# Pinning the weights' sums behind the evictions on VectorE, and issuing a row's end behind the next row's sum in the last product

## The chip, the core and the metric

The kernel runs on one core of one Trainium2 chip. The core has a matrix engine (PE, TensorE), three engines for elementwise work (DVE or VectorE, ACT or ScalarE, POOL or GpSimd), a queue for transfers (SP), an on-chip memory SBUF of 128 partitions, and PSUM, the memory into which PE writes its sums. Each engine works through its own instructions in the order in which they were laid out when the kernel was built; semaphores hold an instruction back until what it reads is there. The metric is the device time of one execution in microseconds, the median of the runs.

## What is computed

A decoder block with two attention branches, a gated merge, a SwiGLU feed-forward and a final RMSNorm, on 1024 tokens of width 1024. The change touches the feed-forward and the final norm alone:

```
h = rmsnorm(x, norm_ffn_g[l])
gu = h @ w_ffn_in[l]                                     # 1024 x 1024 times 1024 x 5632
x = x + (silu(gu[..., :D_FF]) * gu[..., D_FF:]) @ w_ffn_out[l]   # D_FF = 2816
return rmsnorm(x, norm_final_g)
```

## The kernel before, in words

All matrix products are made to float32 accuracy from three passes: each operand is split into a part `hi` and a remainder `lo`, and hi·hi, lo·hi and hi·lo are added in PSUM. `split` (L100 to L102) makes `hi` on ACT (L101) and then `lo = src - hi` on DVE or POOL (L102).

**The first feed-forward product** (L1002 to L1207) works in 22 feature blocks `f` of 128 columns. A block's gate weights `g` and up weights `u` are two rows of 128 x 1024 in SBUF, loaded by `load_f` (L921). A block needs four quarter products per output; a scheme of Strassen's kind makes them from seven products of half size, in the order of `SEQ`: A11, S2, A12, S3, S1, A22, S4. Here A11, A12 and A22 are halves of the loaded weights, and S1 to S4 are sums of them:

```
1028  V.tensor_add(S1, u, d["A22"])
1029  V.tensor_sub(S2, S1, d["A11"])
1030  V.tensor_sub(S3, d["A11"], u)
1031  V.tensor_sub(S4, d["A12"], S2)
```

These are "the weights' sums", four VectorE operations of 128 x 512 on SBUF per block. They are written in `prep`, which the loop calls four products ahead; so the sums of block f+1 stand in the code behind product S1 of block f and its eviction (L1082). Each product's weights are then split: `hi` on ACT into a tile `ahi`, `lo` on POOL into `alo`; there are six of each.

A product is twelve matmuls of 128 x 512 (four slices, three passes) on L1061. Its result is evicted by `product_out`: A11 by ACT (L1070), A12 by ACT as a Silu (L1076), and by DVE S2 (L1073), S3 (L1079), S1 (L1082), A22 (L1085, then the multiplication L1086) and S4 (L1090, then Silu on ACT L1091 and the multiplication L1092). Three PSUM banks take part: A11 and A12 add into `mm`; S2, S3 and A22 into `tr`; S1 and S4 into `big`. A later product of a bank adds to what the earlier one left there, and the earlier state has to be read first: S3 can't start before L1073 has read S2, nor A22 before L1079, nor S4 before L1082. Between the two there is one product of another bank.

After each odd block, `sums` (L1104 to L1107) makes four more sums on DVE, of the two blocks' activations, and SP stores them. In each odd block POOL also makes four sums of the second product's weights (`tsums`, L1123 to L1126), whose place is fixed.

**The second feed-forward product** (L1273 to L1302) runs in 77 units of twelve matmuls (L1277). The last of its seven passes (p = 6) finishes token rows 0 to 3: the last three units run row by row, nine matmuls a row; `evict` adds the result to the residual (L1261), `square` takes the sum of squares on ACT (L1220), and `finish` adds two halves of it (L1225), forms the inverse root on DVE (L97) and POOL (L98), scales one half of the row on ACT (L1229) and the other on DVE (L1230), and issues two stores (L1232).

**What sets the order.** A scheduler lays out each engine's instructions when the kernel is built, by its own estimates of when their operands are ready; so an instruction can stand earlier or later on its engine than in the code. `tc.keep_in_program_order(...)` around an instruction forbids that for it: it stays behind what the code issued before it on its engine.

Of the kernel before, what the change touches and what calls it, by code (L numbers as in the profile page):

```python
# [50 lines left out]
def block_kernel(ctx, tc, x, pos, g_mix, w_qk, w_v, q_scale, w_idx, w_gate, ikg, ikb, lams, sub_g, gate_b,  # L51
                 w_bdsa, w_bdiff, w_out, g_ffn, w_ffi, w_ffo, g_fin, out):
    nc = tc.nc
    V, A, G, T = nc.vector, nc.scalar, nc.gpsimd, nc.tensor
# [39 lines left out]
    def rsqrt(dst, ssq, n, eps):  # L94
        k = ssq.shape[-1]
        v = small.tile([P, NT], F32, name="rs_v")
        V.tensor_scalar(v[:, :k], ssq, 1.0 / n, eps, op0=OP.mult, op1=OP.add)  # L97
        G.tensor_tensor(dst, v[:, :k], nhalf[:, :k], op=OP.pow)  # L98

    def split(hi, lo, src, lo_eng):  # L100
        A.activation(hi, src, AF.Copy)  # L101
        lo_eng.tensor_sub(lo, src, hi.bitcast(F32))  # L102
# [676 lines left out]
    for h in range(4):  # L779
        for j, t in enumerate(ORDER):  # L780
            u = Unit()
# [5 lines left out]
    for m in range(8):  # L787
        prs = {}
        for j, t in enumerate(ORDER2):
            u = Unit()  # L790
# [9 lines left out]
    for i in range(len(units) + 9):  # L800
        if i < len(units) and units[i].first:
            u = units[i]
# [6 lines left out]
        for lag in range(10):  # L809
            if 0 <= i - lag < len(units):  # L810
                u = units[i - lag]
# [51 lines left out]
    class Space:  # L863
# [26 lines left out]
        def drop(self, *aps):  # L890
            for ap in aps:
                self.free += self.of.pop(id(ap))[1]
# [4 lines left out]
    def blk(early):  # L897
        if early:
            return b1p.tile([P, 2, 4, 512], F32R, name="blk", bufs=2)
        return b2p.tile([P, 2, 4, 512], F32R, name="blk", bufs=5)  # L900

    def row4(src):
        t = full()
        nc.sync.dma_start(t, bass.AP(tensor=src.tensor, offset=src.offset, ap=[[0, P], [1, D]]))
        return t
# [111 lines left out]
    def prep(n, early=False):  # L1017
        if n >= len(plan):
            return
        f, (a_, _, _) = plan[n]  # L1020
        if f not in src_:
            g, u = raws[f]
            src_[f] = dict(A11=g[:, :512], A12=g[:, 512:], A22=u[:, 512:], own=[g, u])
        d = src_[f]
        if a_[0] == "S" and "S2" not in d:
            S1, S2, S4 = (half_() for _ in range(3))
            S3 = u = d["own"][1][:, :512]
            V.tensor_add(S1, u, d["A22"])  # L1028
            V.tensor_sub(S2, S1, d["A11"])
            V.tensor_sub(S3, d["A11"], u)  # L1030
            V.tensor_sub(S4, d["A12"], S2)
            d.update(S1=S1, S2=S2, S3=S3, S4=S4)
            d["own"] += [S1, S2, S4]
        if early:
            t = W3.pool.tile([P, 1024], F32R, name="raw", bufs=2)
            hi, lo = t[:, :512], t[:, 512:]
        else:
            hi = arp.tile([P, 512], F32R, name="ahi", bufs=6)
            lo = arp.tile([P, 512], F32R, name="alo", bufs=6)
        split(hi, lo, d[a_], G)  # L1040
        wops[n] = hi, lo
        if a_ == "S4":
            drop(*d["own"])
# [93 lines left out]
    def load_u(n):  # L1137
        if n >= len(unit) or n in uraw:
            return
        p, j = unit[n]  # L1140
        a_, b_ = SEQ2[p]
        lo_, hi_ = slice(0, 512), slice(512, 1024)
        sa = {"A11": act_dr[2 * j][:, lo_], "A12": act_dr[2 * j + 1][:, lo_], "A22": act_dr[2 * j + 1][:, hi_],
              "S1": s_dr[j][0], "S2": s_dr[j][1], "S3": s_dr[j][2], "S4": s_dr[j][3]}[a_]
        sb = {"B11": w_ffo[2 * j][:, lo_], "B21": w_ffo[2 * j + 1][:, lo_], "B22": w_ffo[2 * j + 1][:, hi_],
              "T1": t_dr[j][0][:, lo_], "T3": t_dr[j][0][:, hi_], "T4": t_dr[j][1][:, lo_],
              "T2": t_dr[j][1][:, hi_]}[b_]
        t = uraw[n] = full()
        nc.sync.dma_start(t[:, :512], sa)
        nc.sync.dma_start(t[:, 512:], sb)  # L1150

    def split_u(n):
        if n >= len(unit) or n in uop:
            return
        if n % 2 == 0:
            ublk[n // 2] = blk(False).rearrange("p a b c -> p (a b c)").rearrange("p (n a c) -> p n a c", n=2, a=2)
        v = ublk[n // 2][:, n % 2]
        split(v[:, 0, :], v[:, 1, :], uraw[n], V)
        drop(uraw[n])
        uop[n] = v  # L1160

    banks, ev = [None] * 3, {}
    prep(0, True)
    prep(1, True)
    half1 = turn2("T2", 0)
    product(0)
# [10 lines left out]
    for n in range(2, 6):  # L1177
        prep(n)
# [30 lines left out]
    def x2_load():  # L1209
        for h in range(2):  # L1210
            v = blk(True).bitcast(F32).rearrange("p a b c -> p (a b c)").rearrange("p (r c) -> p r c", r=4)
            for r in R:
                x2[4 * h + r] = v[:, r, :]
                nc.sync.dma_start(x2[4 * h + r], x2_dr[4 * h + r])

    def square(i, u):
        if i not in sqs:
            sqs[i] = small.tile([P, 2], F32, name="ssq2")
        junk = half_()
        A.activation(junk, x2[i][:, u * 512:u * 512 + 512], AF.Square, accum_out=sqs[i][:, u:u + 1])  # L1220
        drop(junk)

    def finish(i):
        sq = sqs[i]
        V.tensor_add(sq[:, 0:1], sq[:, 0:1], sq[:, 1:2])  # L1225
        r = small.tile([P, 1], F32, name="rstd")
        rsqrt(r, sq[:, 0:1], D, EPS)

        A.activation(x2[i][:, :512], x2[i][:, :512], AF.Copy, scale=r)  # L1229
        V.scalar_tensor_tensor(x2[i][:, 512:], x2[i][:, 512:], r, gfin[:, 512:], op0=OP.mult, op1=OP.mult)  # L1230
        for u in range(2):
            nc.sync.dma_start(out[i * P:(i + 1) * P, u * 512:u * 512 + 512], x2[i][:, u * 512:u * 512 + 512])  # L1232

    def evict(p, r, X):
        L, H = slice(0, 512), slice(512, 1024)
        if p == 0:
            pA[r] = half_()
            A.activation(pA[r], X, AF.Copy)
        elif p == 1:
            V.tensor_add(x2[r][:, L], X, x2[r][:, L])  # L1240
            square(r, 0)
            G.tensor_mul(x2[r][:, L], x2[r][:, L], gfin[:, L])
        elif p == 2:
            u2[r] = half_()
            V.tensor_add(u2[r], X, pA[r])  # L1245
            G.tensor_add(u2[r], u2[r], x2[r][:, H])
        elif p == 3:
            u3[r] = half_()
            V.tensor_add(u3[r], X, pA[r])
            G.tensor_add(u3[r], u3[r], x2[4 + r][:, H])  # L1250
            G.tensor_add(pA[r], pA[r], x2[4 + r][:, L])
        elif p == 4:
            V.tensor_add(x2[4 + r][:, L], X, pA[r])
            square(4 + r, 0)
            G.tensor_mul(x2[4 + r][:, L], x2[4 + r][:, L], gfin[:, L])
        elif p == 5:
            V.tensor_add(x2[4 + r][:, H], X, u3[r])
            square(4 + r, 1)
            finish(4 + r)
        else:  # L1260
            V.tensor_add(x2[r][:, H], X, u2[r])  # L1261
            square(r, 1)
            finish(r)

    def bank_set(k):
        if k:
            return [b[:, u, :] for b in (big_bank(), big_bank()) for u in range(2)]
        return [mm_bank(), mm_bank()] + [tr_bank().rearrange("p a b -> p (a b)") for _ in range(2)]
# [4 lines left out]
    def unit_mm(n, r):  # L1273
        p, j = unit[n]
        v = uop[n]
        for m, (a, b) in enumerate(PASS):
            T.matmul(bs_[r], lhsT=v[:, a, r * P:(r + 1) * P], rhs=v[:, b, 512:],  # L1277
                     start=p in OPEN and j == 0 and m == 0, stop=p in SHUT and j == NP - 1 and m == 2,
                     skip_group_check=True)
# [3 lines left out]
    for n, (p, j) in enumerate(unit):  # L1283
        if j == 0 and p in OPEN:
            bs_ = bank_set(p == 2)
        if n == 2:
            x2_load()
            gfin = row4(g_fin)
        if n < len(unit) - TAILU:
            for r in R:  # L1290
                unit_mm(n, r)
                if j == NP - 1:
                    evict(p, r, bs_[r])
        elif n == len(unit) - TAILU:
            for r in R:
                for m in range(n, len(unit)):
                    unit_mm(m, r)
                evict(p, r, bs_[r])
        split_u(n + SA)
        load_u(n + LA)  # L1300

# [74 lines left out]
```

## Time and profile before

| | us |
|---|---|
| median of 3 runs | 1628.11 (1628.06, 1628.11, 1634.58) |
| the profiled execution | 1631.66 |
| span of its records | 1629.6 |
| of it PE busy | 1549.3 (95%) |
| of it DVE busy | 1165.1 (71%) |
| of it POOL busy | 570.4 (35%) |
| first feed-forward product (from 956 to 1407) | 450.9 |
| second feed-forward product with its last row (from 1407) | 222.5 |

The page shows PE as nearly always busy. What is to be read is where it is not: the view of waits names, for each stretch in which PE stood still, the line that released it; the view in order of time, one engine at a time, shows what that engine did before. In that view a row gives start, duration, engine, line, operation, `out<-in` by the program's names, the size, how many like it follow each other, and in brackets how long the engine had been idle and what ended the idling. Names of rows of SBUF are cut to `r`.

### The profile page before, as it was taken

Reading aid. Unit: us, or ns where it says so; the run is one execution under the profiler, and the core shown is the slowest. Engines: PE = TensorE matmul, PEld = TensorE weight load, DVE = VectorE, ACT = ScalarE, POOL = GpSimd, SP = SyncE. Lnnn points to the kernel's source line nnn. Section 1 sums busy time; section 2 is a strip of 40 time slices with the busy share of each in tenths; the row PEclk is TensorE's granted clock in tenths of the full one; section 3 lists DMA queues with packets and bytes.
Section 4 is the critical chain, followed back from the end, with each engine's and each line's share of the span. In section 5 each row is a group of like instructions: output and inputs, shape, how many; then the busy total and the mean of one; then the engine's idle time right before and its main releaser. Section 6 shows DMA issues by size and latency. Waiting matters only on the chain. (4 is left out here: it accounts for less than half of the span.)

```text
span 1629.6 us, 22639 instructions
## 1 busy us (share of the span) xinstructions
PE 1549.3 (95%) x8204; PEld 1319.4 (81%) x8204; DVE 1165.1 (71%) x1880; ACT 670.2 (41%) x1199; POOL 570.4 (35%) x465
## 2 busy tenths in 40 slices
PE   7799999999999998899999989999999999999997
PEld 6688779998888787788788977788787878887886
DVE  6479999989999998788772377555555555745553
ACT  5444541222211887777831243233232322443343
POOL 2442611342210024222421126666566666203311
PEclk9899999999999999999999999999999999999999
DMA  5243243348521466775384132444344445885532
GB/s 173 80 142 119 84 148 123 100 140 230 144 91 52 104 140 146 185 194 158 136 283 169 40 116 107 154 163 165 136 168 153 165 154 194 313 317 181 168 130 104
DMA packets 108079, 247.45 MB, mean 152 GB/s; under 512 B 12480, under 2 KB 30016, under 8 KB 107968
## 3 DMA queue, kind: packets, MB, share of 16 engines
q1 hardware_dynamic: 107968, 246.02, 46.2%
q8 instruction: 64, 1.05, 0.3%
q14 instruction: 47, 0.39, 0.1%
HBM read 167.06 MB, written 78.91 MB: 151 GB/s over the span
## 5 line engine op out<-in xcount | busy, mean ns | idle before, releaser
L102 POOL TENSOR_TENSOR alo<-r,ahi 128x512 fp32r<-128x512 f32 x152 | 206.4, 1366 | 165.3 <-ACT ahi L101 159.7
L102 POOL TENSOR_TENSOR wlo<-raw,whi 128x1024 fp32r<-128x1024 f32 (+1 forms) x49 | 117.5, 2404 | 310.0 <-ACT whi L101 300.6
L101 ACT ACTIVATE ahi<-r 128x512 fp32r<-128x512 f32 x152 | 95.5, 631 | 259.7 <-PE tr L1061 88.1
L1061 PE MATMUL tr<-blk,ahi 128*128 128x512 f32 x528 | 165.4, 394 | 9.2 <-DVE r L1073 8.5
L299 DVE MAX8 m<-score 128x8 f32<-128x640 f32 (+5 forms) x176 | 162.6, 924 | 5.4 <-POOL score L283 0.4
L300 DVE MATCH_REPLACE8 score<-m,score 128x640 f32<-128x640 f32 (+5 forms) x176 | 159.5, 906 | 0.0
L102 DVE TENSOR_TENSOR blk<-r,blk 128x1024 fp32r<-128x1024 f32 x77 | 101.6, 1352 | 73.8 <-ACT blk L101 73.6
L101 ACT ACTIVATE whi<-raw 128x1024 fp32r<-128x1024 f32 (+1 forms) x52 | 53.5, 1032 | 202.7 <-issue 97.7
L1061 PEld LDWEIGHTS tr<-blk,ahi 128*128 128x128 f32 x528 | 98.8, 189 | 33.6 <-DVE r L1073 11.9
L101 ACT ACTIVATE blk<-r 128x1024 fp32r<-128x1024 f32 x77 | 78.1, 1053 | 108.4 <-PE big L1277 44.4
L1061 PE MATMUL big<-blk,ahi 128*128 128x512 f32 x352 | 109.1, 391 | 0.9 <-DVE blk L102 0.9
L427 PE MATMUL mm<-hT_hi,whi 128*128 128x512 f32 x256 | 102.2, 399 | 5.6 <-DVE st_lo L489 5.6
L1061 PE MATMUL mm<-blk,ahi 128*128 128x512 f32 x336 | 104.3, 391 | 0.4 <-ACT r L1070 0.3
L1061 PE MATMUL tr<-blk,alo 128*128 128x512 f32 x264 | 103.6, 393 | 0.6 <-POOL alo L102 0.6
L427 PE MATMUL mm<-hT_lo,whi 128*128 128x512 f32 x256 | 100.6, 393 | 0.0
L427 PE MATMUL mm<-hT_hi,wlo 128*128 128x512 f32 x256 | 100.3, 392 | 0.0
L427 PE MATMUL big<-hT_hi,whi 128*128 128x512 f32 x256 | 99.6, 389 | 0.0
L427 PE MATMUL big<-hT_lo,whi 128*128 128x512 f32 x256 | 99.6, 389 | 0.0
L427 PE MATMUL big<-hT_hi,wlo 128*128 128x512 f32 x256 | 99.6, 389 | 0.0
L1277 PE MATMUL big<-blk 128*128 128x512 f32 x396 | 91.8, 391 | 1.8 <-DVE r L1245 1.5
L1277 PEld LDWEIGHTS big<-blk 128*128 128x128 f32 x396 | 73.8, 188 | 19.5 <-issue 1.9
L592 PE MATMUL big<-khs,qs 128*128 128x512 f32 (+4 forms) x192 | 74.4, 389 | 5.3 <-DVE mx L701 2.5
(286 smaller groups left out, 3973.9 us busy)
## 6 DMA issues: line engine op xcount, KB each, us to landing
r<-in_w_ffi_dram SPq DMA_DIRECT2D x44, 512.0 KB, 4.5
r<-in_w_ffo_dram SPq DMA_DIRECT2D x22, 512.0 KB, 4.8
tdr<-r SPq DMA_DIRECT2D x22, 512.0 KB, 2.6
sdr<-r SPq DMA_DIRECT2D x44, 256.0 KB, 2.6
r<-sdr SPq DMA_DIRECT2D x44, 256.0 KB, 4.0
r<-tdr SPq DMA_DIRECT2D x44, 256.0 KB, 4.0
r<-actdr SPq DMA_DIRECT2D x33, 256.0 KB, 4.1
r<-in_w_ffo_dram SPq DMA_DIRECT2D x33, 256.0 KB, 5.2
```

The lines of the kernel that those rows point to most:

```text
L101: A.activation(hi, src, AF.Copy)
L102: lo_eng.tensor_sub(lo, src, hi.bitcast(F32))
L299: tc.keep_in_program_order(V.max(m8, work[t]))
L300: V.match_replace(work[t], m8, work[t], GONE)
L427: T.matmul(dst, lhsT=w[b][:, k * P:(k + 1) * P], rhs=hT[a][:, k, u * 512:(u + 1) * 512], start=n == 0, stop=n == 23)
L592: T.matmul(sp_[:, u, :n], lhsT=q[:, t * P:(t + 1) * P], rhs=kh_[:, cols], start=True, stop=False)
L1061: T.matmul(banks[z], lhsT=w[b][:, k * P:(k + 1) * P], rhs=o[:, a, k, :], start=first and m == 0, stop=last and m == 11, skip_group_check=True)
L1277: T.matmul(bs_[r], lhsT=v[:, a, r * P:(r + 1) * P], rhs=v[:, b, 512:], start=p in OPEN and j == 0 and m == 0, stop=p in SHUT and j == NP - ...
```

## The change

The first of the four weights' sums, L1028, is kept in program order; L1029 and L1031 read what it or its follower wrote. The addition at the head of `finish`, L1225, is kept in program order too. In the last pass `finish(r)` is no longer called in row r's eviction: `finish(r - 1)` is called behind it, and `finish(3)` after the loop.

```diff
         if a_[0] == "S" and "S2" not in d:
             S1, S2, S4 = (half_() for _ in range(3))
             S3 = u = d["own"][1][:, :512]
-            V.tensor_add(S1, u, d["A22"])
+            tc.keep_in_program_order(V.tensor_add(S1, u, d["A22"]))
             V.tensor_sub(S2, S1, d["A11"])
...
     def finish(i):
         sq = sqs[i]
-        V.tensor_add(sq[:, 0:1], sq[:, 0:1], sq[:, 1:2])
+        tc.keep_in_program_order(V.tensor_add(sq[:, 0:1], sq[:, 0:1], sq[:, 1:2]))
...
             V.tensor_add(x2[r][:, H], X, u2[r])
             square(r, 1)
-            finish(r)
+            if r:
+                finish(r - 1)
...
                 evict(p, r, bs_[r])
+            finish(3)
```

How the order changes. On DVE, in the first feed-forward product, the end of an odd block and the even block behind it, before (row names carry buffer numbers here; `tr`, `mm` and `big` are the PSUM banks; L1028 to L1031 on `r_8905`, `r_8898` are the sums of the next even block, those on `r_8901`, `r_8904` the sums of the odd block after that):

```order
L1107 TENSOR_TENSOR r_8900<-r_8898,r_8905 128x512
L1073 TENSOR_TENSOR r_8894<-tr,r_8897 128x512
L1079 TENSOR_TENSOR r_8895<-tr,r_8897 128x512
L1082 TENSOR_TENSOR r_8895<-big,r_8895 128x512
L1028 TENSOR_TENSOR r_8899<-r_8905 128x512
L1029 TENSOR_TENSOR r_8899<-r_8899,r_8898 128x512
L1030 TENSOR_TENSOR r_8905<-r_8898,r_8905 128x512
L1085 TENSOR_TENSOR r_8907<-tr,r_8897 128x512
L1031 TENSOR_TENSOR r_8908<-r_8898,r_8899 128x512
```

So the sums of an even block stood in the even block before it, one block earlier than in the code. Those of the odd block came next, around L1073 of the odd block before, and their last one behind L1086:

```order
L1092 TENSOR_TENSOR r_8907<-r_8907,r_8895 128x512
L1028 TENSOR_TENSOR r_8894<-r_8901 128x512
L1029 TENSOR_TENSOR r_8897<-r_8894,r_8904 128x512
L1073 TENSOR_TENSOR r_8895<-tr,r_8893 128x512
L1030 TENSOR_TENSOR r_8901<-r_8904,r_8901 128x512
L1079 TENSOR_TENSOR r_8900<-tr,r_8893 128x512
L1082 TENSOR_TENSOR r_8900<-big,r_8900 128x512
L1085 TENSOR_TENSOR r_8906<-tr,r_8893 128x512
L1086 TENSOR_TENSOR r_8906<-r_8906,r_8896 128x512
L1031 TENSOR_TENSOR r_8893<-r_8904,r_8897 128x512
```

Now, on DVE, the same odd block:

```order
L1073 TENSOR_TENSOR r_8895<-tr,r_8893 128x512
L1079 TENSOR_TENSOR r_8900<-tr,r_8893 128x512
L1082 TENSOR_TENSOR r_8900<-big,r_8900 128x512
L1028 TENSOR_TENSOR r_8899<-r_8905 128x512
L1029 TENSOR_TENSOR r_8899<-r_8899,r_8898 128x512
L1030 TENSOR_TENSOR r_8905<-r_8898,r_8905 128x512
L1031 TENSOR_TENSOR r_8908<-r_8898,r_8899 128x512
L1085 TENSOR_TENSOR r_8906<-tr,r_8893 128x512
L1086 TENSOR_TENSOR r_8906<-r_8906,r_8896 128x512
L1090 TENSOR_TENSOR r_8895<-big,r_8895 128x512
L1092 TENSOR_TENSOR r_8906<-r_8906,r_8900 128x512
L1104 TENSOR_TENSOR r_8908<-r_8907,r_8906 128x512
```

In every block, even or odd, the next block's four sums now stand together between L1082 and L1085; behind L1104 follow L1105 to L1107 and the next even block's L1073, as before. POOL's order is as before: behind `tsums` of an odd block come the `lo` of S2, A12, S3, S1, A22 and S4 of the even block behind it, then that of A11 of the next odd one. On ACT the split of the next block's S2 now stands behind L1076, where it stood ahead of it.

On DVE, at the end of the kernel, the rows 0 to 3 now:

```order
L1261 TENSOR_TENSOR blk<-mm,r_8900 128x512 x2
L1225 TENSOR_TENSOR ssq_13630<-ssq_13630 128x1
L97 TENSOR_SCALAR rs_v<-ssq_13630 128x1
L1230 SCALAR_TENSOR_TENSOR blk<-blk,rstd,r_8901 128x512
L1261 TENSOR_TENSOR blk<-tr,r_8896 128x512
L1225 TENSOR_TENSOR ssq_13637<-ssq_13637 128x1
L97 TENSOR_SCALAR rs_v<-ssq_13637 128x1
L1230 SCALAR_TENSOR_TENSOR blk<-blk,rstd,r_8901 128x512
L1261 TENSOR_TENSOR blk<-tr,r_8896 128x512
```

Before, row 0's L1225, L97 and L1230 stood between the two first L1261, and row 3's L1261 behind all three earlier rows' L1230; now each L1261 stands ahead of the end of the row before it.

## Rows read from the trace of the kernel before

**Rows 1.** First feed-forward product: span, busy PE, PEld, DVE, ACT, POOL, clock, DMA share, GB/s.

```profile
956.18:1407.07 450.89, 436.10 (x1925) 354.47 (x1926) 265.44 (x311) 148.25 (x237) 273.46 (x198) 1.00 0.44 159
```

**Rows 2.** What PE waited for: us in total, times, longest.

```profile
PE tr L1061 <- DVE r L1073: 8.5, 8, 2.0
...
PE tr L1061 <- DVE r L1079: 0.3, 1, 0.3
```

**Rows 3.** PE in order of time, where S3 of an odd block starts.

```profile
1080.33 0.73 PE L1061 MATMUL tr<-blk,ahi 128*128 128x512 f32 x2 [0.45 <-DVE r L1073]
```

**Rows 4.** DVE in order of time, an odd block and the next one's start.

```profile
1077.29 0.69 DVE L1028 TENSOR_TENSOR r<-r 128x512 f32<-128x512 f32 x1 [2.92 <-DMA r<-in_w_ffi_dram]
1078.07 1.60 DVE L1029 TENSOR_TENSOR r<-r,r 128x512 f32<-128x512 f32 x1
1079.60 0.68 DVE L1073 TENSOR_TENSOR r<-tr,r 128x512 f32<-128x512 f32 x1
...
1086.11 0.69 DVE L1082 TENSOR_TENSOR r<-big,r 128x512 f32<-128x512 f32 x1 [2.03 <-PE big L1061]
1088.83 0.69 DVE L1085 TENSOR_TENSOR r<-tr,r 128x512 f32<-128x512 f32 x1 [2.03 <-PE tr L1061]
1089.62 1.59 DVE L1086 TENSOR_TENSOR r<-r,r 128x512 f32<-128x512 f32 x1
...
1091.74 0.68 DVE L1090 TENSOR_TENSOR r<-big,r 128x512 f32<-128x512 f32 x1
1093.11 0.82 DVE L1092 TENSOR_TENSOR r<-r,r 128x512 f32<-128x512 f32 x1 [0.70 <-ACT r L1091]
...
1094.69 0.69 DVE L1105 TENSOR_TENSOR r<-r,r 128x512 f32<-128x512 f32 x1
1095.30 1.78 DVE L1106 TENSOR_TENSOR r<-r 128x512 f32<-128x512 f32 x1
1097.01 0.68 DVE L1107 TENSOR_TENSOR r<-r,r 128x512 f32<-128x512 f32 x1
1097.61 0.68 DVE L1073 TENSOR_TENSOR r<-tr,r 128x512 f32<-128x512 f32 x1
1102.43 0.69 DVE L1079 TENSOR_TENSOR r<-tr,r 128x512 f32<-128x512 f32 x1 [4.14 <-PE tr L1061]
```

**Rows 5.** POOL in order of time, the same stretch.

```profile
1085.21 3.77 POOL L102 TENSOR_TENSOR alo<-r,ahi 128x512 fp32r<-128x512 f32 x3
1089.37 1.30 POOL L102 TENSOR_TENSOR alo<-r,ahi 128x512 fp32r<-128x512 f32 x1 [0.38 <-ACT ahi L101]
...
1094.81 1.73 POOL L102 TENSOR_TENSOR alo<-r,ahi 128x512 fp32r<-128x512 f32 x1 [1.42 <-ACT ahi L101]
```

**Rows 6.** ACT in order of time, the same stretch.

```profile
1088.66 0.63 ACT L101 ACTIVATE ahi<-r 128x512 fp32r<-128x512 f32 x1 [2.10 <-PE tr L1061]
...
1092.45 0.63 ACT L1091 ACTIVATE r<-r 128x512 f32<-128x512 f32 x1 [0.44 <-DVE r L1090]
```

**Rows 7.** DVE in the second feed-forward product, operations of 128 x 1024.

```profile
1503.57 2.36 DVE L102 TENSOR_TENSOR blk<-r,blk 128x1024 fp32r<-128x1024 f32 x2 [2.84 <-ACT blk L101]
...
1530.74 4.36 DVE L102 TENSOR_TENSOR blk<-r,blk 128x1024 fp32r<-128x1024 f32 x2 [0.41 <-ACT blk L101]
```

**Rows 8.** POOL beside the second of them.

```profile
1531.75 2.27 POOL L1251 TENSOR_TENSOR r<-r,blk 128x512 f32<-128x512 f32 x1
```

**Rows 9.** DVE in order of time, the last four token rows.

```profile
1614.00 0.69 DVE L1261 TENSOR_TENSOR blk<-mm,r 128x512 f32<-128x512 f32 x1 [15.21 <-PE mm L1277]
1615.54 0.16 DVE L1225 TENSOR_TENSOR ssq<-ssq 128x1 f32<-128x1 f32 x1 [0.85 <-ACT r L1220]
...
1616.56 0.76 DVE L1230 SCALAR_TENSOR_TENSOR blk<-blk,rstd,r 128x512 f32<-128x512 f32 x1 [0.67 <-POOL rstd L98]
...
1622.53 0.68 DVE L1261 TENSOR_TENSOR blk<-tr,r 128x512 f32<-128x512 f32 x1
...
1625.02 0.75 DVE L1230 SCALAR_TENSOR_TENSOR blk<-blk,rstd,r 128x512 f32<-128x512 f32 x1 [0.67 <-POOL rstd L98]
```

## The prediction, made before the changed kernel ran

> **What bounds the kernel now.** First the busy time by stages: in the first feed-forward product PE is busy 436.10 of 450.89 us [rows 1], so its matmuls set the time there and the idle 14.8 us are all that an order can give back. Next the waits of PE: the one that comes back is S3 waiting for L1073, 8.5 us in 8 waits, the longest 2.0; L1079 adds 0.3 [rows 2]. Last the order in time, to see what kept L1073. In the odd block of rows 4 the sums of a later block stood in front of it: L1028 began at 1077.29 after 2.92 us of waiting for weights, L1029 took 1.60, L1073 began at 1079.60 [rows 4], and S3 at 1080.33, 0.45 late [rows 3]. So L1073 starts 0.73 before the S3 that it releases. One end of one PE product and the next are 2.72 us apart (L1082 at 1086.11, L1085 at 1088.83, each at once behind its product) [rows 4].
>
> At the even block there is no such stall, but little room. S3 of the even block ended at about 1102.23 (L1079 at 1102.43, 0.20 behind, like the others), so it began at 1102.23 - 2.72 = 1099.51, and L1073 may start as late as 1099.51 - 0.73 = 1098.78. It started at 1097.61 [rows 4]: **1.17 us of slack**, at the end of an uninterrupted run of VectorE from L1092 on.
>
> **What VectorE and GpSimd cost each other.** An operation of VectorE that reads SBUF alone takes 0.68 to 0.69 (L1105, L1107), and begins 0.60 behind the one before (L1106 at 1095.30, if it needs nothing from it: 0.61 after L1105). L1106 itself took 1.78 [rows 4]. Beside it POOL's `lo` began at 1094.81, while L1105 was still to run, and took 1.73 instead of 1.30 [rows 5]. It ended at 1096.54; L1106 ended at 1097.08, 0.54 later. And POOL's operation ended 1.16 after L1105's end at 1095.38. So the two take turns, none goes twice while the other waits, and a turn costs VectorE 1.16 + 0.54 = **1.70 instead of 0.60**. The same where both have a queue: two operations of 128 x 1024 took 4.36 instead of 2.36, while POOL's took 2.27 [rows 7, 8]. Evictions, which read PSUM, stay at 0.68 to 0.69 [rows 4].
>
> The Trainium skill, page "SBUF — State Buffer", section "Who interferes with whom", has a rule for this that speaks against the change: a VectorE instruction with two SBUF inputs contends with a GpSimd instruction that reads SBUF, and whichever issued first holds the shared ports for the whole instruction. The rows agree on who blocks whom. Held for the whole of the recorded durations, 0.68 + 1.30, a turn would be 1.98; by the sum below that would make the kernel some 1651 us.
>
> **The change part by part.**
>
> *What it removes.* L1028 to L1031 no longer stand in front of L1073, in any block. The 8.5 us go, with the 0.3 of L1079, which the same queue held up: **-8.8 us**.
>
> *What it moves.* All four sums of the next block now stand between L1082 and L1085. In an odd block they were made earlier, so POOL could begin the `lo` of S2 directly behind `tsums`: three `lo` from 1085.21 to 1088.98 (1.26 each), then one every 2.72 us, at PE's pace [rows 5]. Now S2 exists only behind L1029, POOL's queue is in order, and the `lo` of S2, A12, S3, S1, A22, S4 and A11 follow each other without a gap, just where L1086, L1092 and L1104 to L1107 want to run. I work it out on the odd block of rows 4, L1082 at 1086.11.
>
> - L1028 1086.71, L1029 0.78 later (the distance to L1029 in rows 4) at 1087.49, L1030 1088.09, L1031 1088.69 to 1089.29.
> - S2's `hi` on ACT 0.71 behind L1029's start (as L1091 at 1092.45 behind L1090 at 1091.74), `lo` 0.71 behind that (1088.66 to 1089.37) [rows 4 to 6]: 1088.91. L1031 is running, so `lo` ends 1.16 after it, at 1090.45.
> - L1085 1089.29; L1086 wants 1090.08, waits for 1090.45, ends 1091.0. `lo` A12 ends 1092.15.
> - L1090 needs S4, the second product behind S1: 1091.55. L1091 0.71 later, L1092 wants to start 0.66 behind that (as in rows 4 and 6), 1092.92. `lo` S3 runs from 1092.15, with no one in front, to 1093.4 (1.26). L1092 ends 1093.95.
> - Four turns of 1.70 for L1104 to L1107, against `lo` of S1, A22, S4, A11 (their `hi` are there: A22 behind S4, S4 behind the even block's A11, A11 behind its S2, by 1097.8 at the latest): 1100.75.
> - L1073 starts at 1100.75 instead of 1097.61, 1.97 after 1098.78.
>
> So S3 of each even block waits some 1.95 us for L1073, where it waited for nothing. There are ten (blocks 2 to 20): **+19.5 us**. What costs nothing: in an even block the same sums end L1092 at the same distance from L1082, 7.84 us, but no L1104 to L1107 follow, and L1073 may start 12.67 behind L1082, so 4.8 us are free; that is also the room for a late `lo` there. The weights' transfers are not late: sums that waited 2.92 us for them stood 1.5 blocks ahead of their place. PE itself needs the `lo` of S2 at 1094.07, and gets it at 1090.45.
>
> Not shown by these rows is the first block, where transposes share PE and the order changes most; VectorE has fewer sums before its evictions and more behind L1082. I take 0, and -1 to +2 for the range, the size of a single wait of PE [rows 2].
>
> *The last rows.* The run-in was: L1261 of row 0 at 1614.00, its L1230 at 1616.56, and for row 3 L1261 at 1622.53 and L1230 at 1625.02 [rows 9]. A row's nine matmuls are 2.04 us (nine twelfths of 2.72), so row 3 can be evicted from 1614.00 + 3 x 2.04 = 1620.12; it stood 2.4 us behind that, in the queue. Now it waits for one L1230 less. Step by step with the same distances: L1261 of rows 0 and 1 at 1614.00 and 1616.04, row 0's L1225 to L1230 until 1618.38, L1261 of row 2, row 1's end until 1620.66, L1261 of row 3, row 2's end until 1622.94, then row 3's L1225, and its L1230 1.02 behind (as from L1225 to L1230 of row 0, with POOL between): 1623.96 instead of 1625.02: **-1.1 us**. The whole 2.4 is not had, since row 2's end now stands in front of row 3's.
>
> **Sum.** 19.5 - 8.8 - 1.1 = +9.6 us. On the profiled execution: 1631.66 + 9.6 = 1641.3. That execution is 3.55 above the median; nothing in the step hangs on it, so the same 9.6 go on the median: 1628.11 + 9.6 = **1637.7**. Bounds: if the chain has one turn fewer (a `lo` arrives late and leaves the way free), the wait is 1.95 - 1.10 = 0.85: 8.5 - 9.9 = -1.4, 1626.7. If a turn costs the undisturbed spacings, 1.26 + 0.60 = 1.86, five turns make 0.8 more: 2.75, 27.5 - 9.9 = +17.6, 1645.7.
>
> **The rivals.**
>
> *The stalls go and none comes* (faster). VectorE keeps its turn when its next operation is ready at once, or POOL's backlog is gone by 1093. Then L1104 to L1107 take 4 x 0.60 behind 1093.95 and L1073 starts by 1096.4, inside the slack. For it: L1105 and L1107 ran undisturbed. Against it: they began while POOL had nothing to do, and L1106, ready directly behind L1105, still lost its turn [rows 4, 5]. The point from which it decides is two turns lost out of the last four: one costs 1.10 and is inside 1.17, two are not. Gain 9.9: **1618.2**.
>
> *The stalls change place and size evenly out* (same). One or two turns less in most pairs, 0 to 0.85 each: between 1618 and 1627, say **1623**.
>
> *Weights become the wait* (slower still). The transfers are issued behind the stores of L1104 to L1107; if these are late, L1028 waits at L1082, in an odd block to the full. The wait of 2.92 [rows 4] ten times: +29, **1667**. Against it: those transfers land a block ahead of the pinned sums.
>
> **How the numbers follow.** Forecast 0.66; stalls gone 0.15; evening out 0.11; weights or another wait 0.08. Predicted is the forecast's 1637.7, its own range 1626.7 to 1645.7. For 8 in 10 the range goes down into the second rival and up to the bound: 1621 to 1646; left out are most of the first rival and the third. A measurement of this kernel can tell about 0.5%, 8.1 us, from no change: faster is below 1620.0, slower above 1636.2. The forecast is slower only if the wait exceeds 1.8 us, which I give 0.42 of its 0.66; with the third rival slower is 0.50. Faster: 0.15 and a little of the second, 0.17. Same: 0.33.
>
> **What would show it.** Right: no wait of PE for L1073 in odd blocks, and ten in even ones, 1.5 to 2.5 each, with L1104 to L1107 at 1.7 each beside an unbroken row of POOL's `lo`; VectorE busier by some 20 to 40 us, since waiting for a turn counts as busy; last L1230 1.1 earlier against the last matmul. Wrong: L1104 to L1107 at 0.69 in odd blocks (then the first rival), or L1028 waiting for a transfer (the third). The weakest step is that POOL has no gap in its seven `lo`.

## The result, and the profile after

The changed kernel takes **1645.84 us** (median of four runs, 1642.47 to 1646.50) beside 1629.18 of the kernel before (four runs, 1628.06 to 1634.58): a ratio of 1.0091, with a 95% interval of 1.0065 to 1.0118. The ratio is taken over all the runs, not from the two medians. It is slower, by 11 to 19 us. A second measurement, of `after_again` below, gives 1.0085 (1.0059 to 1.0111). Its profiled execution is 1642.47 us with a span of 1640.8, where that of before had 1631.66 and 1629.6.

| between the two profiled executions | us |
|---|---|
| up to the first feed-forward product (956.59 before, 955.69 after) | -0.9 |
| first product (450.3, now 462.2) | +11.9 |
| second product (213.2, now 214.5) | +1.3 |
| last matmul's end to the last L1230 (4.94, now 3.79) | -1.15 |
| span | +11.2 |

The first product is counted from its first matmul to the first of the second product; the stretch of [rows 1] begins 0.4 us earlier and ends 0.2 later. All of the loss lies there. First that product as a whole, in the columns of [rows 1] (span, busy PE, PEld, DVE, ACT, POOL, clock, DMA share, GB/s):

```profile
955.69:1417.93 462.24, 439.06 (x1923) 357.71 (x1922) 267.15 (x308) 144.59 (x237) 288.18 (x198) 0.99 0.43 151
```

DVE's busy time has hardly moved (267.15 beside 265.44), POOL's has grown by 14.7, and the clock reads 0.99 instead of 1.00. What PE waited for there (us in total, times, longest) answers to [rows 2]:

```profile
PE tr L1061 <- DVE r L1073: 18.2, 10, 1.8
...
PE tr L1061 <- ACT ahi L101: 1.6, 1, 1.6
```

L1079 is gone from the list, and the waits for L1073 are ten of 1.8 in place of eight of up to 2.0. In order of time they stand at 1021.09, 1061.30, 1101.51 and so on, at S3 of blocks 2, 4, ... 20, and none in an odd block. The third of them in the order of PE:

```profile
1099.30 0.39 PE L1061 MATMUL mm<-blk,alo 128*128 128x512 f32 x1
1101.51 0.73 PE L1061 MATMUL tr<-blk,ahi 128*128 128x512 f32 x2 [1.82 <-DVE r L1073]
```

The 1.82 is counted from the end of the matmul before, at 1099.69. In an unbroken row the matmuls start 0.23 apart, so without the wait S3 would have started at 1099.53: it was held back by 1.98.

Now DVE in the odd block ahead of it, which answers to [rows 4]:

```profile
1086.12 0.69 DVE L1082 TENSOR_TENSOR r<-big,r 128x512 f32<-128x512 f32 x1 [2.03 <-PE big L1061]
1086.73 0.68 DVE L1028 TENSOR_TENSOR r<-r 128x512 f32<-128x512 f32 x1
...
1089.32 0.68 DVE L1085 TENSOR_TENSOR r<-tr,r 128x512 f32<-128x512 f32 x1
1090.11 1.00 DVE L1086 TENSOR_TENSOR r<-r,r 128x512 f32<-128x512 f32 x1
...
1092.96 1.11 DVE L1092 TENSOR_TENSOR r<-r,r 128x512 f32<-128x512 f32 x1 [0.70 <-ACT r L1091]
1094.16 1.61 DVE L1104 TENSOR_TENSOR r<-r,r 128x512 f32<-128x512 f32 x1
1095.87 1.59 DVE L1105 TENSOR_TENSOR r<-r,r 128x512 f32<-128x512 f32 x1
1097.39 1.78 DVE L1106 TENSOR_TENSOR r<-r 128x512 f32<-128x512 f32 x1
1099.09 1.76 DVE L1107 TENSOR_TENSOR r<-r,r 128x512 f32<-128x512 f32 x1
1100.77 0.68 DVE L1073 TENSOR_TENSOR r<-tr,r 128x512 f32<-128x512 f32 x1
```

and POOL beside it, which answers to [rows 5]:

```profile
1089.00 11.30 POOL L102 TENSOR_TENSOR alo<-r,ahi 128x512 fp32r<-128x512 f32 x7 [3.72 <-ACT ahi L101]
```

Each of the four sums L1104 to L1107 now takes 1.6 to 1.8 us, where three of the four took 0.69 and one 1.78 before [rows 4]; beside them POOL's seven subtractions follow each other without a gap from 1089.00 to 1100.30. L1073 stands directly behind and starts 3.2 us later against L1082 (14.65 behind it, before 11.50).

Last the clock, in a window behind the stall at 1141.70 and in the next (span, busy PE, granted clock, DMA share, GB/s):

```profile
1141.50:1145.00 3.50, 3.30 (x8) 0.55 0.83 275
1145.50:1149.00 3.50, 3.50 (x17) 1.00 0.88 338
```

In the first window the clock is at its lower level, 1.2 instead of 2.4 GHz, for nearly all of it, and PE makes 8 matmuls there, against 17 in the same time behind. The order of PE shows it matmul by matmul:

```profile
1141.70 1.12 PE L1061 MATMUL tr<-blk,ahi 128*128 128x512 f32 x2 [1.82 <-DVE r L1073]
1142.62 0.63 PE L1061 MATMUL tr<-blk,alo 128*128 128x512 f32 x1
...
1145.45 0.62 PE L1061 MATMUL tr<-blk,ahi 128*128 128x512 f32 x2
1145.91 0.39 PE L1061 MATMUL tr<-blk,alo 128*128 128x512 f32 x1
```

A matmul of 0.39 takes 0.63. Of the nine distances from one of the ten stalls to the next, six are 40.19 to 40.21 us and three 41.81 or 41.82: those with such a stretch behind the first of the two stalls (1141.70, 1263.89 and 1345.91). So **one slow stretch costs 1.62 us** on top of the stall. The stall itself costs 2.12 us: two blocks take 38.08 us in `asums_pinned` below, which has none of these stalls (S3 of two even blocks at 1096.94 and 1135.02), and 40.20 here. A fourth slow stretch of the product, from 971.2 to 974.6, stands in the run-in (the product's first block, in which transposes share PE), behind the wait of 1.6 for ACT in the list above; the kernel before has one in the whole product, at 1160.8.

### The profile page after: what moved, and what is told of

The parts are those of the page before. It is cut to its first block, busy times and chain, and to the rows that moved or that the text cites. A ratio compares the mean times of both kernels' runs of the same rounds, so it can differ in the third digit from the quotient of the medians.

```text
span 1640.8 us, 22661 instructions
## 1 busy us (share of the span) xinstructions
PE 1552.4 (95%) x8204; PEld 1322.6 (81%) x8204; DVE 1167.4 (71%) x1880; ACT 667.0 (41%) x1199; POOL 586.2 (36%) x465
## 5 line engine op out<-in xcount | busy, mean ns | idle before, releaser
L102 POOL TENSOR_TENSOR alo<-r,ahi 128x512 fp32r<-128x512 f32 x152 | 229.0, 1541 | 163.7 <-ACT ahi L101 162.2
L1061 PE MATMUL tr<-blk,ahi 128*128 128x512 f32 x528 | 169.5, 402 | 19.8 <-DVE r L1073 18.2
L101 ACT ACTIVATE ahi<-r 128x512 fp32r<-128x512 f32 x152 | 88.6, 625 | 242.6 <-DVE r L1029 166.4
L1278 PEld LDWEIGHTS big<-blk 128*128 128x128 f32 x396 | 73.8, 188 | 19.5 <-issue 1.9
```

The lines of the kernel that those rows point to most:

```text
L1061: T.matmul(banks[z], lhsT=w[b][:, k * P:(k + 1) * P], rhs=o[:, a, k, :], start=first and m == 0, stop=last and m == 11, skip_group_check=True)
```

## The experiments

The theory: VectorE's operations that read SBUF alone and POOL's take turns; with the sums pinned, POOL's seven subtractions lie beside the four sums L1104 to L1107, each of these costs a whole turn, and L1073 behind them is late. The rivals: the part in the last product has a share in it; it is only the length of VectorE's queue, without POOL; and, for what the unprofiled runs lie above the profiled one, other waits than those of the profile. Each kernel was measured beside runs of the kernel before.

| kernel | us | ratio to before | 95% interval |
|---|---|---|---|
| `sums_only` | 1648.93 | 1.0124 | 1.0099 to 1.0150 |
| `finish_only` | 1629.76 | 1.0004 | 0.9987 to 1.0020 |
| `one_turn_less` | 1619.87 | 0.9942 | 0.9921 to 0.9963 |
| `two_lo_less` | 1615.98 | 0.9930 | 0.9907 to 0.9954 |
| `sums_at3` | 1625.54 | 0.9976 | 0.9958 to 0.9993 |
| `sums_at2` | 1618.50 | 0.9931 | 0.9910 to 0.9953 |
| `asums_pinned` | 1617.08 | 0.9927 | 0.9904 to 0.9951 |
| `asums_only` | 1659.54 | 1.0168 | 1.0141 to 1.0195 |
| `after_again` | 1645.14 | 1.0085 | 1.0059 to 1.0111 |

The kernel before had 1629.71, 1629.95 and 1630.68 beside the first four, the next three and the last two.

### The two parts apart

`sums_only` is the kernel before with this alone:

```
-            V.tensor_add(S1, u, d["A22"])
+            tc.keep_in_program_order(V.tensor_add(S1, u, d["A22"]))
```

> Only the pin on the weights' sums, the last product's row ends as before. Theory (the pin alone brings the ten new stalls, through turns of VectorE and POOL): ten stalls of 1.8 us at S3 of the even blocks, none in the odd ones, and a tail as before, 4.9 us from the last matmul's end to the last L1230 (3.8 in the changed kernel). The time is then that of the changed kernel plus 1.1: 1643 to 1648 us. Rival (the two parts work together, the later row ends hold space back that the first product wants): fewer or shorter stalls, and a time within 4 us of the kernel before.

It has all of the loss, 1648.93, and the same ten waits, 18.2 us in all, the longest 1.8. Its last L1230 starts 4.93 us behind the last matmul's end. It lies 3.1 us above the changed kernel, where 1.1 were expected, and 0.9 above the expected range. The intervals of the two overlap; the profile of `sums_only` has five slow stretches behind its stalls, where that of the changed kernel has three.

`finish_only` is the rest of the change: L1225 kept in program order, `finish(r - 1)` behind row r's sum, `finish(3)` after the loop, and L1028 free.

> Only the part in the last product (a row's end behind the next row's sum); the weights' sums float as before. Theory: the odd blocks' stalls of 8.5 us in all are there as before, no stall at the even blocks' S3, and the tail from the last matmul's end to the last L1230 is 3.8 us in place of 4.9: 1.1 us under the kernel before, 1627 us beside 1628. Rival (this part costs): the kernel before plus 2 us or more.

No difference in time: 1.0004, so the expected 1.1 us can't be told from none. The tail itself is 3.78 us instead of 4.94, as in the changed kernel, so its 1.15 us are there; they are below what these runs can tell (0.2% is 3 us). The odd blocks' waits are back:

```profile
PE tr L1061 <- DVE r L1073: 9.8, 8, 3.2
```

So the pin alone makes the ten stalls, and the other part neither adds to them nor takes from them.

### Is it turns, or only the queue?

`one_turn_less` is the changed kernel without one of the four sums; what it leaves out is S3 of the activations:

```
-        V.tensor_sub(S3, a0[:, :512], S3)
```

> The changed kernel without the third of the four sums behind an odd block (L1106, S3 of the activations; its output is left out and what stands in the row goes out in its place). Theory (each of the four sums costs a turn of 1.7 us with a POOL instruction): L1073 comes 1.70 us earlier, the ten stalls shrink from 1.82 to some 0.1 us each, 18.2 to about 1, and the time falls by 17 us and more below the changed kernel's, as far as the granted clock falls less often: 1621 to 1627 us. Rival (the sum only takes its own 0.60 us of VectorE's queue): stalls of 1.2 us, 12 in all, and 6 us less than the changed kernel: 1637 to 1640 us.

`two_lo_less` leaves VectorE's work as it is and takes two of POOL's seven subtractions away; the low parts of A12 and S3 of each even block are left out:

```
-        split(hi, lo, d[a_], G)
+        if f and f % 2 == 0 and a_ in ("A12", "S3"):
+            A.activation(hi, d[a_], AF.Copy)
+            lo = hi
+        else:
+            split(hi, lo, d[a_], G)
```

> The changed kernel with the low parts of A12 and S3 of each even block left out (the high part stands in for them), so that POOL has five subtractions in place of seven beside the odd block's last VectorE instructions; VectorE's own work and its order are those of the changed kernel. Theory: POOL is then idle in some of the stretch, two of the four sums run in 0.6 us in place of 1.7, L1073 comes at least 2 us earlier and the ten stalls are gone (under 0.2 us each): 1620 to 1626 us. Rival (the length of VectorE's queue alone makes the stall, POOL has no part): ten stalls of 1.8 us as in the changed kernel, 1642 to 1646 us.

In both the list of waits has none for S2's eviction in the first product, and both are faster than expected, by 1.1 and 4.0 us below the ranges' ends. One sum less gave 1619.87, not the 1637 to 1640 that its 0.60 us of the queue would give. The three sums left in `one_turn_less` still take a turn each, and L1073 follows L1082 (at 1080.17) by 12.97 instead of 14.65: a whole turn of 1.68 has gone with a sum whose own place in the queue is 0.60.

```profile
1088.20 1.61 DVE L1104 TENSOR_TENSOR r<-r,r 128x512 f32<-128x512 f32 x1
...
1093.14 0.68 DVE L1073 TENSOR_TENSOR r<-tr,r 128x512 f32<-128x512 f32 x1
```

S3 starts 0.73 behind it, at 1093.87, and so is still held back, by 0.3 us, which is too short for the list. Two subtractions less on *another engine* gave 1615.98, with nothing changed on VectorE but its speed. Here is POOL in `two_lo_less`, beside an odd block's end and an even block's start:

```profile
1083.52 4.52 POOL L102 TENSOR_TENSOR alo<-r,ahi 128x512 fp32r<-128x512 f32 x3 [3.67 <-ACT ahi L101]
1089.40 1.29 POOL L102 TENSOR_TENSOR alo<-r,ahi 128x512 fp32r<-128x512 f32 x1 [1.36 <-ACT ahi L101]
1092.11 1.49 POOL L102 TENSOR_TENSOR alo<-r,ahi 128x512 fp32r<-128x512 f32 x1 [1.41 <-ACT ahi L101]
```

and DVE; four lines have come in above, so the sums are L1108 to L1111 and S2's eviction is L1077:

```profile
1088.68 0.69 DVE L1108 TENSOR_TENSOR r<-r,r 128x512 f32<-128x512 f32 x1
1089.48 1.77 DVE L1109 TENSOR_TENSOR r<-r,r 128x512 f32<-128x512 f32 x1
1091.17 0.68 DVE L1110 TENSOR_TENSOR r<-r 128x512 f32<-128x512 f32 x1
...
1092.38 0.68 DVE L1077 TENSOR_TENSOR r<-tr,r 128x512 f32<-128x512 f32 x1
```

Where POOL is idle, a sum takes 0.68 and the next begins 0.60 behind it; the one that meets a subtraction takes 1.77. The rival of the bare queue falls. In both kernels the clock has its lower level nowhere between the run-in and the end of the first product.

### Ways out of the turns

Two ways keep all the work and all the outputs. `sums_at3` and `sums_at2` make the weights' sums of the next block one or two products earlier, ahead of L1082 or of L1079, so that POOL starts earlier. `wsums` holds L1028 to L1031, pinned as in the changed kernel; in `sums_at2` the condition is `j == 2`:

```
         product(n)
+        if j == 3 and 0 < f < NF - 1:
+            wsums(raw_ops(f + 1))
         prep(n + AHEAD)
```

> The changed kernel with the weights' sums of the next block one product earlier: pinned ahead of L1082 (the eviction of S1), not behind it. All work and all outputs as in the changed kernel. Theory: S2's sum is ready 2.6 us earlier, POOL starts its seven subtractions that much or more earlier and is done with them before the third or fourth of the odd block's sums, so L1073 comes at least the missing 1.82 us earlier: the ten stalls go (under 2 us in all), the granted clock falls less often in the first product, and the time is 1614 to 1620 us, 9 to 16 us under the kernel before. Rival (the weights' rows: the sums take their three half rows earlier, the next weights' transfers start later and become the wait): L1028 idle behind a transfer, 1625 us or more.

> The same, two products earlier: pinned ahead of L1079 (the eviction of S3). In the changed kernel's trace the weights' last row was issued 1077.45 and takes some 5 us to land, and L1079 stood at 1083.41 in the odd block. Theory: the stalls at the even blocks' S3 go as with one product earlier, and the sums wait up to 1 us for the transfer with room behind them (L1079 has 2.0 us until L1082): 1614 to 1621 us. Rival (too early: the sums wait for the transfer and L1079 and L1082 behind them, PE waits in the odd blocks for the bank or the low parts): stalls of 1 us or more in the odd blocks, 1625 us or more.

`sums_at2` did as expected: 1618.50, and the wait for S2's eviction has gone; one wait of 1.0 for S3's is left, in block 1. `sums_at3` went half way, and its expectation missed: it has ten waits of 0.4 to 0.7 left, 5.3 us where I had under 2 (six lines have come in above; L1079 is S2's eviction there):

```profile
PE tr L1067 <- DVE r L1079: 5.3, 10, 0.7
```

The reason stands in its order of DVE: the sums begin 2.6 us earlier, but the first of them now meets the last of POOL's `tsums` and loses 1.0 of it, and two of the four sums of the activations still lose their turn, with L1098 (the multiplication ahead of them).

```profile
1084.10 1.68 DVE L1026 TENSOR_TENSOR r<-r 128x512 f32<-128x512 f32 x1
...
1093.04 1.81 DVE L1098 TENSOR_TENSOR r<-r,r 128x512 f32<-128x512 f32 x1 [0.70 <-ACT r L1097]
...
1095.68 1.59 DVE L1111 TENSOR_TENSOR r<-r,r 128x512 f32<-128x512 f32 x1
...
1097.80 1.77 DVE L1113 TENSOR_TENSOR r<-r,r 128x512 f32<-128x512 f32 x1
```

`sums_at3` takes 7 us more than `sums_at2`, and its waits for S2's eviction are 5.3. In the two profiles 2.3 of the 7.1 us lie ahead of the first product, where neither edit reaches, and 4.8 in it.

`sums_at2` has more turns than any kernel so far. Of the weights' sums, the multiplication L1086 (L1092 here) and the activations' sums, 59 take over 1.4 us, where the changed kernel has 40. In its odd blocks all four of the weights' sums lose one, this time to POOL's last subtraction and to `tsums`. But they stand where there is room: S3's eviction behind them, L1085, comes late, and the product that it releases is held back by less than 0.2 us (it starts at 1083.33, 0.40 behind the matmul before instead of 0.23).

```profile
1075.88 1.69 DVE L1026 TENSOR_TENSOR r<-r 128x512 f32<-128x512 f32 x1
...
1080.90 1.77 DVE L1029 TENSOR_TENSOR r<-r,r 128x512 f32<-128x512 f32 x1
1082.60 0.68 DVE L1085 TENSOR_TENSOR r<-tr,r 128x512 f32<-128x512 f32 x1
```

`asums_pinned` leaves the weights' sums where the change put them and takes the four sums of the activations out of L1073's way, behind it:

```
     elif a_ == "S2":
         ev["u2"] = half_()
         V.tensor_add(ev["u2"], X, ev["p1"])
+        if f and f % 2 == 0:
+            sums(f // 2 - 1)
...
-            if f % 2:
+            if f == NF - 1:
                 sums(f // 2)
...
-        V.tensor_add(S1, S3, a1[:, 512:])
+        tc.keep_in_program_order(V.tensor_add(S1, S3, a1[:, 512:]))
```

> The changed kernel with the four sums of the activations (L1104 to L1107) behind the next block's L1073, pinned there, not ahead of it. All outputs as in the changed kernel; only the last block has its sums where they were. Theory: the queue ahead of L1073 loses its four turns (6.8 us), L1073 waits for PE alone, the ten stalls go, the four sums run behind it in VectorE's idle time: 1614 to 1621 us. Rival (the sums' rows are held longer, so that the next weights' transfers start later, or the sums now make L1079 or L1028 late): stalls elsewhere in the even blocks, 1625 us or more.

1617.08, **the fastest of those that keep all the work**, though not to be told from `sums_at2` by these intervals; 0.7% below the kernel before and some 26 to 29 us below the changed one. PE waits for no eviction of S2, S3 or S1. The order of DVE (two lines have come in above the sums, which are L1106 to L1109):

```profile
1090.37 1.11 DVE L1094 TENSOR_TENSOR r<-r,r 128x512 f32<-128x512 f32 x1 [0.70 <-ACT r L1093]
1094.49 0.69 DVE L1073 TENSOR_TENSOR r<-tr,r 128x512 f32<-128x512 f32 x1 [3.01 <-PE tr L1061]
1095.10 1.83 DVE L1106 TENSOR_TENSOR r<-r,r 128x512 f32<-128x512 f32 x1
1096.97 0.69 DVE L1107 TENSOR_TENSOR r<-r,r 128x512 f32<-128x512 f32 x1
```

and of POOL:

```profile
1086.42 9.97 POOL L102 TENSOR_TENSOR alo<-r,ahi 128x512 fp32r<-128x512 f32 x7 [3.71 <-ACT ahi L101]
```

L1073 now waits 3.01 us for PE, not PE for it. In that time POOL works its seven subtractions off, in 9.97 us instead of 11.30, and is nearly through when the sums come: one of them loses a turn, three take 0.69.

### The pin without its harm, and the harm without the pin

`asums_only` is `asums_pinned` with L1028 free again.

> As the kernel with the activations' sums behind the next block's L1073, but without the pin on the weights' sums (L1028 floats as in the kernel before). Theory (the pin's own part is to take the odd blocks' stalls away): in odd blocks L1028 to L1030 stand again in front of L1073 and PE waits there 5 to 10 us in all; nothing in the even blocks: 1621 to 1628 us. Rival (with the four sums out of the way the pin is worth nothing): odd stalls under 2 us, 1614 to 1619 us.

Both sides missed: 1659.54, the slowest of all. PE waits for evictions as the theory said, but 25.7 us in all where I had 5 to 10 (L1084 is S1's eviction there):

```profile
PE tr L1061 <- DVE r L1073: 14.2, 6, 2.8
...
PE big L1061 <- DVE r L1084: 11.5, 3, 3.9
```

Free, L1028 and its followers stand in front of an eviction again, and beside POOL's subtractions they take a turn each:

```profile
1073.86 1.78 DVE L1028 TENSOR_TENSOR r<-r 128x512 f32<-128x512 f32 x1
1075.67 1.66 DVE L1030 TENSOR_TENSOR r<-r,r 128x512 f32<-128x512 f32 x1
1077.26 1.75 DVE L1029 TENSOR_TENSOR r<-r,r 128x512 f32<-128x512 f32 x1
1078.93 0.68 DVE L1073 TENSOR_TENSOR r<-tr,r 128x512 f32<-128x512 f32 x1
```

or wait for a place in SBUF to come free, at which L1084 stands behind them:

```profile
1127.69 1.47 DVE L1028 TENSOR_TENSOR r<-r 128x512 f32<-128x512 f32 x1 [4.21 <-DMA tdr<-r]
```

The matmuls run at 0.63 behind eight of its nine waits. Its first product is 30.9 us longer than before: 16.8 are waits, and nine more slow stretches of 1.62 make 14.6. So the two edits don't add up (both kernels here also hold the change in the last product, which made no difference in `finish_only`): against the kernel before, the pin alone loses 1.2% (`sums_only`), the later sums alone 1.7%, and both together gain 0.7%.

### What the unprofiled runs have more

`after_again` is the changed kernel, unaltered.

> The changed kernel once more, unaltered, for the granted clock. Theory (the unprofiled runs lie above the profiled one because stalls of 1.8 us are followed by a stretch at half clock, in a number that changes from run to run): ten stalls of 18.2 us in all, as before to 0.1; n stretches at half clock in the first product behind stalls, each 1.62 us longer than at full clock; the span is 1640.8 + 1.62 (n - 3), within 3 us; mean clocks of 0.984 to 0.988, where the kernel before has 0.989 to 0.991. Rival (the waits themselves differ from run to run): the sum of the waits for L1073 is not 18.2, or the span is off by more than 3 us.

The waits are the same, ten and 18.2 us. Matmuls of 0.63 stand behind five of the ten stalls (three in the first profile), so the span should be 1640.8 + 2 x 1.62 = 1644.0; it is 1644.6. That it comes so near is partly luck. The slow stretch in the run-in of the first profile is not there in the second, so the first product has five in place of four, and it is 1.60 longer (463.84 beside 462.24), which is one stretch. Of the other 2.2 us of the span 1.9 lie ahead of the first product, and the theory says nothing of them. The first product of `sums_only`, with five slow stretches too, takes 463.85. The other runs of both measurements have mean clocks of 0.984 to 0.988 and times of 1642.69 to 1646.84; the kernel before has 0.988 to 0.991 in this comparison. So the price of a slow stretch is shown by three profiles. That such stretches make the whole of what the unprofiled runs have more is not shown: of these runs only the mean clock is known, and it doesn't order them (1643.99 at 0.985, 1646.84 at 0.987).

## Why the prediction was right, and where it fell short

**The sign and the mechanism** were right, in the place that was named: slower, by ten stalls at S3 of the even blocks.

**What it removes**, 8.8 us: right. No wait for L1073 or L1079 is left in an odd block.

**What it moves**, 19.5 us: 18.2 in the list of waits. The chain came out within 0.2: S2's `lo` at 1089.00 (worked out 1088.91), L1104 at 1094.16 (1093.95), L1073 at 1100.77 (1100.75). The four turns took 1.71, 1.52, 1.70 and 1.68, where I had 1.70 each. That each stall reads 0.13 shorter than the forecast's 1.95 is the way of counting: the forecast went from start to start, the list counts from the end of the matmul before. S3 was held back by 1.98, and the slower start behind a wait (0.73 for two matmuls instead of 0.62) brings the loss to some 2.1. The 8.8 taken off were counted by the list, so the sum mixed the two ways; with some 0.3 more for each wait on both sides its difference changes little. The turns are 1.65 on the mean. Held for the whole of the recorded durations, 0.68 + 1.30, they would be 1.98, and for the undisturbed spacings, 0.60 + 1.26, 1.86. The Trainium skill says that VectorE with two SBUF inputs contends with a GpSimd instruction that reads SBUF (page "SBUF — State Buffer", section "Who interferes with whom"), and these rows agree. The Trainium skill also says that whichever starts first has the pair of ports for the whole instruction (same page, section "SBUF: two separate sides"); the 1.65 is less than that gives by either count.

**The weakest step**, that POOL has no gap in its seven subtractions, held: one row of seven, 11.30 us. `two_lo_less` shows that it was the step on which all hung: with two gaps the time is that of the first rival, 1618.2 there and 1615.98 here.

**The last rows**, -1.1: -1.15. Too small to be seen in the time.

**The first block**, 0: its waits changed; the one for ACT's split grew from 0.5 to 1.6. Of the first product's 11.9, 9.4 are the waits as listed (18.2 - 8.8) and 4.9 the three slow stretches more (four beside one), so -2.4 is left for the rest of the run-in and what I can't place. Against `asums_pinned`, which has none of these stalls and no slow stretch in this product (434.63 us), all is placed: ten stalls of 2.12 and four slow stretches of 1.62 make 27.7 us, and the changed kernel has 27.6 more. The second product's +1.3 was not foreseen; 0.74 of it are two waits for an eviction by ACT (L1238; 0.47 at 1448.48, 0.27 at 1450.40).

**The size** was short. The profiled execution came out at 1642.47 where the sum gives 1641.3, but the median at 1645.84 where I said 1637.7: 8.1 too few. Three parts make that up. 1.2 is the sum itself. 3.55 is the profiled execution of before over the median of its three runs, which I carried over with the words "nothing in the step hangs on it"; with 18 and 20 runs the kernel before has medians of 1629.7 and 1630.0, so that median was some 1.6 low. 3.4 is the median of after over its profiled run. **The step that fell short is the one from the profiled execution to the median**, with a missing term in the sum: a stall costs PE more than its own time if the clock falls behind it. In the profile that was four stretches against one before (three behind the new stalls, one in the run-in), +4.9, hidden there by 3.7 less in the rest of the first product; `after_again` has five. Whether the other runs' 3.4 are such stretches is not shown. The forecast's own range ended at 1645.7, 0.1 below the median, and had no room for them, since its upper end was worked out from turns alone; that the wider range, to 1646, holds the median is luck, since it was not turns of 1.86 us that took the time.

**What would show it**: the forecast that VectorE would be busier by 20 to 40 us was wrong. Its busy time is 1167.4 us instead of 1165.1, and in the first product 267.15 instead of 265.44. The turns had been there before; I had counted only those that the change brings. In the groups of DVE (busy us, mean ns, idle time) the kernel before had

```profile
L1086 DVE TENSOR_TENSOR r<-r,r 128x512 f32<-128x512 f32 x22 | 30.0, 1363 | 1.1
L1030 DVE TENSOR_TENSOR r<-r,r 128x512 f32<-128x512 f32 x22 | 26.5, 1203 | 0.0
...
L1104 DVE TENSOR_TENSOR r<-r,r 128x512 f32<-128x512 f32 x11 | 7.6, 693 | 0.3
...
L1107 DVE TENSOR_TENSOR r<-r,r 128x512 f32<-128x512 f32 x11 | 7.5, 681 | 0.0
```

and the changed one

```profile
L1086 DVE TENSOR_TENSOR r<-r,r 128x512 f32<-128x512 f32 x22 | 21.9, 994 | 2.1
...
L1107 DVE TENSOR_TENSOR r<-r,r 128x512 f32<-128x512 f32 x11 | 18.3, 1664 | 0.0
...
L1104 DVE TENSOR_TENSOR r<-r,r 128x512 f32<-128x512 f32 x11 | 16.7, 1521 | 1.0
...
L1030 DVE TENSOR_TENSOR r<-r,r 128x512 f32<-128x512 f32 x22 | 15.1, 686 | 0.0
```

Of the operations L1028 to L1031, L1086 and L1104 to L1107 in the first product, 44 took over 1.4 us before and 40 do now. **The change made no turns; it gathered them**, from places with room to one place in front of an eviction on which PE waits.

**The rivals.** The first (stalls go, none comes) did not happen, but its time is what one gets once the turns are out of the way. The third (weights become the wait) was seen nowhere in the changed kernel; L1028 waits for a transfer in none of its 22 places.

## What to carry to other kernels

When an instruction is pinned to free one engine's queue, follow its output to the next engine in order: what has to be read is what now runs beside what, and in front of which release. A lost turn costs something only where the loser has an operation behind it on which PE waits: `sums_at2` has 59 long operations of VectorE and takes 1618.50 us, the changed kernel has 40 and takes 1645.84. So move the operations that nobody waits for (here the activations' sums) behind the release, as `asums_pinned` does, or make the others where there is room, as `sums_at2` does; these runs can't tell which is better. And one pin by itself can lose what two pins win: measure them together as well as apart.

## What the runs showed of the hardware that was not expected

A stall of TensorE costs more than the list of waits says, and at times it is paid twice. A stall listed with 1.82 us costs 2.12 (40.20 us for two blocks beside 38.08 in `asums_pinned`). And behind three to five of ten such stalls the granted clock went to its lower level, a matmul took 0.63 us instead of 0.39, and 1.62 us more were lost; which of the ten it was is not the same in the two profiles of the changed kernel (the fourth, seventh and ninth; the second, third, fifth, seventh and ninth). In the kernel before it was behind one stall (1.99 us, at 1159.53) and not behind another of 1.95. The ten waits of 0.4 to 0.7 in `sums_at3` had none behind them.
